# Attention's first head, late gates, late weights, merge weights and column sums rearranged

## The chip, the cores and the metric

One core of one Trainium2 chip runs one transformer block. Five engines work side by side, each through its own queue of instructions in order: TensorE (PE, with its weight loads PEld), VectorE (DVE), ScalarE (ACT), GpSimd (POOL) and SyncE (SP), which here only issues transfers; POOL issues some too. The metric is device time in microseconds of the whole program: before the change, the median of 3 runs is 1717.37 us (1715.96 to 1721.29).

## The reference

A block over 1024 tokens of width 1024, in float32: a modulated norm, a token mixer with two branches, and a convolutional feed-forward part. The mixer is what the change touches.

```python
proj = u @ w_in
p_fox, p_rwkv, p_gate = _split(proj, (FOX_COLS, RWKV_COLS, GATE_COLS))
...
o_fox = fox_attention(to_heads(q), to_heads(k), to_heads(v), log_f)    # 8 heads of 64, causal, softmax of
                                                                       # q k / 8 + cum_q - cum_k
o_rwkv = rwkv7_time_mix(p_rwkv, ...)
gate_fox, gate_rwkv = jnp.split(jax.nn.sigmoid(p_gate), N_BRANCHES, axis=-1)
merged = gate_fox * (o_fox @ fox_w_out) + gate_rwkv * (o_rwkv @ rwkv_w_out)
return merged @ w_o
```

After it come `h + gate1 * mix`, a second modulated norm whose shift and scale are columns of `silu(c) @ w_mod`, and the feed-forward part.

## The kernel before

**Products.** A float32 matrix is kept as two float32r parts, `hi` (a rounded copy) and `lo` (what is left). A product is hi hi + hi lo + lo hi, so a gate tile of 128 columns over 512 tokens is 3 x 8 = 24 matmuls of 128x128 by 128x512. `load_w` (line 243) loads a weight tile into `raw` and splits it into `hi` and `lo`: a cast on ACT and two subtractions on DVE, or, while `weave.late` is 1, a cast and four subtractions on POOL. `raw`, `whi` and `wlo` have two buffers each.

**Order.** PE's order is written out by hand for the whole kernel. The class `Weave` does this: it keeps a clock of its own (`now`), runs chains of generators when they are due, and in the time between takes products from a list of fillers (`step`, `fill`). `hold` keeps the filler back for a time, `use` keeps count of what ACT and DVE have to do. In attention (the block `manual_schedule` behind line 1021) DVE and ACT are also in program order; SP and POOL are ordered by a scheduler at build time, in the whole mixer. Transfers wait in the queue of the engine that issues them.

**Stages around the change.** The RWKV branch is worked through first, with `qk`, `v` and gate products (`gt`) as fillers. Its last steps are group norms in `head_sums` (products `mu` and `va` with the constant `blk_r`, splits `Ztr`, `Mtr`, `Zts`, `Mts` on ACT and POOL). When its pools `shp` and `rw` close, the pools `fxp` (eight tiles `h0` to `h7` of 4096 bytes a partition, for attention's output `fx`) and `at` (attention's tiles) open in the same memory, at addresses in the order in which tiles are first asked for. `shp` holds the constants `cst2`, the tiles `sh` and small columns; `blk_r` is the first tile of `rw`.

**Attention.** `load_head` brings one head from memory in three transfers on POOL's queue: `stA` (q and k, 2 x 128 rows), `stB` (their low parts and the decay sums, 2 x 68 rows) and `vh`. Three chains run: `s_chain` makes logits (`lg`, for each block of 128 queries: products with stA, stB and a causal mask), behind which `softmax` takes the row maximum (DVE, L1062), the exponential (ACT, L1066), and scales by the reciprocal of the sum (DVE, L1071 and L1072); `t_chain` transposes P (`tp`) and `halve` splits it into `th` (ACT) and `tl` (DVE, L1102); `a_chain` multiplies with v (`ov`), and `collect` adds the two halves (ACT L1133, DVE L1135) and splits a finished pair into `fx` (POOL L1142 and L1143, for the last head ACT and DVE). The fillers in this stage are the seven gate weights that are left, "late gates": two halves each, in one PSUM bank `rk_ps`. `gate_out` evicts a half: Abs and Relu from PSUM, Exp, Ln on ACT, an addition on DVE, Exp on ACT, then a write to `d_gate`. `s_chain` begins with a wait of 10,500 ns of the planner's clock, in which fillers run.

**Merge and output.** `br_open` loads and splits a merge weight (`raw_br`; `hi_br` on ACT, `lo_br` on POOL) in a pool `br` over attention's memory, `br_part` multiplies and applies the gates. Then `wo_mm` multiplies by `w_o`, eight steps `kt`. At `kt` 4 `mod_2` runs: 2 x 8 one-column products (`mps`; float32, so two matmuls each) that sum the columns for the second norm's shift and scale.

## Time and profile before

| | |
|---|---|
| runs | 1715.96, 1717.37, 1721.29 us |
| span of the profiled execution, first to last instruction | 1713.2 us (its own time is not listed) |
| mean granted clock of PE | 0.986 |
| late gate products `rk_ps` | 336 matmuls, 668.1 to 868.2 us from the span's start |
| first and last logits | 683.3 and 863.2 us |
| merge products `br` | from 877.6 us |
| output products `wo` | from 965.0 us |

Times in views are microseconds from the start of the span unless marked ns. A row of instructions gives the line, the engine, output and input tiles without buffer numbers, their shape and count; then busy time, mean ns of one, and idle time of that engine just before it with what ended most of it. The granted clock is the share of full speed that PE was given. L140 is the line of the helper that issues every matmul, so PE's work is told apart by tiles.

### The profile page before, as it was taken

How to read it: one execution, taken by the hardware profiler on the slowest of the kernel's cores; microseconds unless marked ns; L12 is line 12 of the kernel's file. 1: busy time of each engine (PE TensorE's matmuls, PEld its weight loads, DVE VectorE, ACT ScalarE, POOL GpSimd, SP SyncE). 2: the span in 40 equal slices, each digit the busy share in tenths (PEclk: the TensorE clock that was granted, in tenths of full speed). 3: DMA queues.
4: the chain of work that ended last, by engine and by line, in shares of the span. 5: the costliest groups of instructions: out<-in, count | busy, mean ns of one | idle time of the engine just before them, and what ended most of it. 6: DMA issues, size and time to landing. Idle time of an engine off the chain costs nothing.

```text
span 1713.2 us, 26506 instructions
## 1 busy us (share of the span) xinstructions
PE 1665.3 (97%) x9984; PEld 1367.0 (80%) x9984; DVE 1213.0 (71%) x2432; ACT 813.1 (47%) x1482; POOL 143.5 (8%) x175
## 2 busy tenths in 40 slices
PE   8899999999999999999999999999999999999998
PEld 7867777787777777888878888888888888888886
DVE  4576687777677632889777734897777777786677
ACT  5364343334344454766652314664444444454455
POOL 0001011111110002323212100000000000000000
PEclk9899999999999999999999999999999999999999
DMA  9287644533333226434268611132333223484463
GB/s 310 89 304 236 185 133 112 140 96 116 95 96 98 85 81 158 135 100 125 75 231 288 255 50 62 57 105 98 106 116 111 93 99 117 149 293 153 123 215 111
DMA packets 135311, 239.87 MB, mean 140 GB/s; under 512 B 39888, under 2 KB 64720, under 8 KB 135184
## 3 DMA queue, kind: packets, MB, share of 16 engines
q1 hardware_dynamic: 127232, 220.94, 39.8%
q0 software_dynamic: 7952, 17.25, 3.7%
q8 instruction: 78, 1.28, 0.3%
q14 instruction: 49, 0.40, 0.1%
HBM read 172.59 MB, written 65.54 MB: 139 GB/s over the span
## 4 chain that ended last, share of the span: by engine, by line
PE 80%; DVE 9%; DMA 4%; ACT 3%; SPq 2%; issue 1%; DVEq 0%; ACTq 0%; POOLq 0%
PE X L140 13%; PE D L140 12%; PE Y L140 6%; PE wo L140 5%; PE gt L140 5%; PE br L140 5%; PE ps_rkv L140 5%; PE qk L140 4%; PE rk_ps L140 4%; PE W L140 3%; PE lg L140 2%; PE ov L140 2%; PE tr L140 2%; PE sp L140 2%; PE tp L144 2%
## 5 line engine op out<-in xcount | busy, mean ns | idle before, releaser
L140 PE MATMUL D<-op,op 128*128 128x512 f32 x924 | 209.8, 389 | 0.0
L140 PEld LDWEIGHTS D<-op,op 128*128 128x128 f32 x924 | 173.3, 188 | 36.3 <-DVE op L1245 0.3
L140 PE MATMUL X<-T_m,S 128*128 128x512 f32 x440 | 107.3, 390 | 0.1
L140 PEld LDWEIGHTS X<-T_m,S 128*128 128x128 f32 x440 | 82.4, 188 | 18.2 <-ACT T_m L1670 0.6
L1244 ACT CAST op<-g 128x512 fp32r<-128x512 f32 x77 | 47.8, 621 | 73.0 <-PE D L140 47.9
L1245 DVE TENSOR_TENSOR op<-g,op 128x512 fp32r<-128x512 f32 x77 | 53.0, 689 | 40.9 <-ACT op L1244 40.8
L1481 DVE SCALAR_TENSOR_TENSOR c<-ab,vec,c 128x512 f32<-128x512 f32 x88 | 65.9, 749 | 19.5 <-ACT c L1484 17.9
L263 DVE TENSOR_TENSOR lo_in<-raw_in,hi_in 128x512 fp32r<-128x512 f32 x84 | 56.4, 706 | 31.6 <-PE gt L140 12.3
L796 DVE TENSOR_TENSOR t<-E,M 128x60 f32<-128x60 f32 (+24 forms) x248 | 56.8, 229 | 29.5 <-DMA M<-sm 24.2
L1445 DVE TENSOR_TENSOR S<-ur,S 128x512 fp32r<-128x512 f32 x66 | 45.5, 691 | 35.6 <-ACT S L1441 35.5
L261 ACT CAST hi_in<-raw_in 128x1024 fp32r<-128x1024 f32 x42 | 43.9, 1047 | 52.5 <-PE ps_rkv L140 17.2
L1441 ACT CAST S<-ur 128x512 fp32r<-128x512 f32 x66 | 41.0, 622 | 55.6 <-DVE ur L1434 30.6
L1445 DVE TENSOR_TENSOR A<-ur,A 128x512 fp32r<-128x512 f32 x64 | 44.0, 688 | 30.9 <-ACT A L1441 30.7
L140 PE MATMUL Y<-T_h,A 128*128 128x512 f32 x264 | 63.5, 389 | 0.0
L140 PE MATMUL Y<-T_h,S 128*128 128x512 f32 x264 | 63.3, 389 | 0.0
L140 PE MATMUL X<-B_b,A 128*128 128x512 f32 x252 | 60.8, 390 | 0.0
L140 PE MATMUL W<-B_f,A 128*128 128x512 f32 x252 | 60.6, 389 | 0.0
L1066 ACT ACTIVATE P<-lg,nm 128x896 f32<-128x896 f32 (+3 forms) x64 | 47.5, 744 | 22.1 <-DVE nm L1062 21.9
L140 PEld LDWEIGHTS Y<-T_h,A 128*128 128x128 f32 x264 | 49.6, 188 | 10.4
L798 DVE TENSOR_TENSOR E<-E,t 128x60 f32<-128x60 f32 (+24 forms) x248 | 53.7, 216 | 5.8
L140 PEld LDWEIGHTS Y<-T_h,S 128*128 128x128 f32 x264 | 49.5, 188 | 10.3
L1441 ACT CAST A<-ur 128x512 fp32r<-128x512 f32 x64 | 39.9, 623 | 34.2 <-PE X L140 31.5
(472 smaller groups left out, 4213.3 us busy)
## 6 DMA issues: line engine op xcount, KB each, us to landing
raw_in<-in_w_in SPq DMA_DIRECT2D x50, 512.0 KB, 3.7
wm<-in_w_mod SPq DMA_DIRECT2D x48, 512.0 KB, 6.5
ur<-in_w_up SPq DMA_DIRECT2D x44, 512.0 KB, 4.0
g<-d_g SPq DMA_DIRECT2D x35, 512.0 KB, 3.9
d_g<-gs SPq DMA_DIRECT2D x44, 256.0 KB, 2.0
d_g<-c SPq DMA_DIRECT2D x33, 256.0 KB, 4.4
d_st<-qh SPq DMA_DIRECT2D x64, 128.0 KB, 2.4
d_gate<-gs SPq DMA_DIRECT2D x32, 256.0 KB, 2.6
```

The lines of the kernel that those rows point to most:

```text
L140: nc.tensor.matmul(o, lhsT, rhs, start=start, stop=stop, skip_group_check=more)
L144: nc.tensor.transpose(o, i, eye)
L261: nc.scalar.copy(hi, raw)
L263: nc.vector.tensor_tensor(lo[:, c : c + NH], raw[:, c : c + NH], f32(hi[:, c : c + NH]), op=ALU.subtract)
L796: tt(tv, E32[:, 0:J, s : s + 1].to_broadcast([128, J, W]), M32[:, s : s + 1, s + 1 : 32].to_broadcast([128, J, W]), op=ALU.mult)
L798: tt(E32[:, 0:J, s + 1 : 32], E32[:, 0:J, s + 1 : 32], tv, op=ALU.add)
L1066: nc.scalar.activation(e[:, 0:n], lg[:, 0:n], AF.Exp, bias=nm[:, 0:1], accum_out=nm[:, 1:2])
L1244: nc.scalar.copy(hi, src)
L1245: tt(lo, src, f32(hi), op=ALU.subtract)
L1441: nc.scalar.copy(hi, src)
L1445: tt(lo, src, f32(hi), op=ALU.subtract)
L1481: stt(c, ab[:, x + hf * NH : x + hf * NH + NH], V("conv_w", 22 * x + i), c, op0=ALU.mult, op1=ALU.add)
```

## The change

Five edits. (1) The first head is loaded by `load_first`: five transfers into five `fxp` tiles in the order h3, h7, h2, h6, h5, and `s_chain` begins after 700 ns rather than 10,500; later heads keep `load_head`. (2) A late gate half is evicted by a tanh of half the product and an identity that halves it and adds 0.5, on ACT alone, with the ACT table set `exp_and_others` loaded ahead of attention and the one with Ln loaded behind it; the second half's output has a tile of its own (`gl`, two buffers). (3) Late weights are split like early ones, on ACT and DVE; POOL's subtraction for `fx` is issued in two pieces of 256. (4) The first two merge weights are loaded into `raw` and split (ACT, DVE) into gate-weight buffers before attention's pools close. (5) The column sums are taken four matmuls at a time between the output products of `kt` 3 to 7.

```diff
-    epsr = cp.tile([128, 3], F32, name="epsr")
+    epsr = cp.tile([128, 4], F32, name="epsr")
+    nc.vector.memset(epsr[:, 3:4], 0.5)
...
+        nc.scalar.copy(hi, raw)
         if weave.late == 1:
-            i = nc.gpsimd.tensor_copy(hi, raw)
-            if "head" in marks:
-                tc.add_manual_dep(i.ins, marks["head"].ins.name, NOSYNC)
-            for c in range(0, n, 256):
-                nc.gpsimd.tensor_tensor(lo[:, c : c + 256], raw[:, c : c + 256], f32(hi[:, c : c + 256]), op=ALU.subtract)
-        else:
-            nc.scalar.copy(hi, raw)
-            for c in range(0, n, NH):
-                nc.vector.tensor_tensor(lo[:, c : c + NH], raw[:, c : c + NH], f32(hi[:, c : c + NH]), op=ALU.subtract)
+            weave.use("ACT", weave.now, 900)
+            weave.use("DVE", weave.now, 1200)
+        for c in range(0, n, NH):
+            nc.vector.tensor_tensor(lo[:, c : c + NH], raw[:, c : c + NH], f32(hi[:, c : c + NH]), op=ALU.subtract)
...
+    def load_first():
+
+        parts = [d_st[0, 0], d_st[0, 1], d_st[0, 2, 0:68, :], d_st[0, 3, 0:68, :], d_v[0].rearrange("p a x -> p (a x)")]
+        tiles = [fxp.tile([128, S], F32R, tag=f"h{t}", name=f"first{t}") for t in (3, 7, 2, 6, 5)]
+        for t, x in zip(tiles, parts):
+            marks["head"] = nc.gpsimd.dma_start(t[0 : x.shape[0], :], x)
+        heads[0] = *tiles[0:4], tiles[4].rearrange("p (a x) -> p a x", x=128)
+
...
-    load_head(0)
+    load_first()
...
-            yield 10500
+            yield 700
...
-                A, B, _ = heads[h]
+                qa, ka, qb, kb, _ = heads[h]
...
-                        mm(lg[:, c0:c1], A[:, 0, qs], A[:, 1, c0:c1], start=True, stop=False)
+                        mm(lg[:, c0:c1], qa[:, qs], ka[:, c0:c1], start=True, stop=False)
...
-                        mm(lg[:, c0:c1], B[0:68, 0, qs], B[0:68, 1, c0:c1], start=False, stop=True)
+                        mm(lg[:, c0:c1], qb[0:68, qs], kb[0:68, c0:c1], start=False, stop=True)
...
-                    nc.gpsimd.tensor_tensor(fx[1][p][:, cs], o, f32(fx[0][p][:, cs]), op=ALU.subtract)
+                    for x in range(2):
+                        c = slice(cs.start + x * 256, cs.start + x * 256 + 256)
+                        nc.gpsimd.tensor_tensor(fx[1][p][:, c], o[:, x * 256 : x * 256 + 256], f32(fx[0][p][:, c]), op=ALU.subtract)
...
-                weave.hold = weave.now + 1000
+                weave.hold = weave.now + 700
...
-            g = gsp.tile([128, NH], F32, tag="sp0", name=f"gs{i}_{hf}")
-            m = at.tile([128, NH], F32, tag="gm", name=f"gm{i}_{hf}", bufs=1)
-            nc.scalar.activation(g, rk_ps, AF.Abs)
-            nc.scalar.activation(m, rk_ps, AF.Relu, scale=-1.0)
-            weave.hold = weave.use("ACT", weave.now, 960) + 210
-            nc.scalar.activation(g, g, AF.Exp, scale=-1.0)
-            nc.scalar.activation(g, g, AF.Ln, bias=1.0)
-            yield weave.use("ACT", weave.now, 960) + 140 - weave.now
-            tt(g, g, m, op=ALU.add)
-            yield weave.use("DVE", weave.now, 600) + 140 - weave.now
-            nc.scalar.activation(g, g, AF.Exp, scale=-1.0)
+            g = (at if hf else gsp).tile([128, NH], F32, tag="gl" if hf else "sp0", name=f"gs{i}_{hf}")
+            nc.scalar.activation(g, rk_ps, AF.Tanh, scale=0.5)
+            weave.hold = weave.use("ACT", weave.now, 480) + 210
+            nc.scalar.activation(g, g, AF.Identity, scale=0.5, bias=epsr[:, 3:4])
             weave.use("ACT", weave.now, 480)
...
+        nc.scalar.preload_act_table_set("exp_and_others")
         weave.run([a_chain(), t_chain(), s_chain()])
         weave.late = 2
         weave.run([drain()])
+    ahead = {}
+    for n in range(2):
+        raw = rp.tile([128, 1024], F32, tag="raw", name=f"raw_br0{n}")[:, 0:NH]
+        nc.sync.dma_start(raw, a["w_br"][n, :, 0:NH])
+        hi, lo = (wp.tile([128, 1024], F32R, tag=t, name=f"{t}_br0{n}")[:, 0:NH] for t in ("whi", "wlo"))
+        nc.scalar.copy(hi, raw)
+        nc.vector.tensor_tensor(lo, raw, f32(hi), op=ALU.subtract)
+        ahead[0, n] = hi, lo
+    use_ln_exp()
     es.close()
...
+        if (x, n) in ahead:
+            g = br.tile([128, S], F32, tag="g", name=f"g{x}_{n}")
+            nc.sync.dma_start(g, d_gate[8 * x + n])
+            opened[x, n] = ahead[x, n], g
+            return
...
+    sums2 = mod_2()
...
             wo_mm(t, kt, ps[t])
+            if kt > 2:
+                for _ in range(2):
+                    next(sums2, None)
         mg_split(1, kt)
-        if kt == 4:
-            for _ in mod_2():
-                pass
```

More of the change, by code (lines that the diff above doesn't have):

```diff
@@ L1011, in load_head @@
         vh = at.tile([128, 8, 128], F32R, tag="vh", name=f"vh{h}")
-        i = nc.gpsimd.dma_start(vh, d_v[h])
-        marks.setdefault("head", i)
-        heads[h] = A, B, vh
-    load_head(0)
+        nc.gpsimd.dma_start(vh, d_v[h])
+        heads[h] = A[:, 0, :], A[:, 1, :], B[:, 0, :], B[:, 1, :], vh
+    load_first()
     while len(weave.queue) > 12:
@@ L1115, in a_chain @@
                     yield from slot(ov_free)
-                vh = heads[h][2]
+                vh = heads[h][4]
                 order = [(0, th), (1, th), (1, tl), (0, tl)] if jj == I else [(0, th), (0, tl), (1, th), (1, tl)]
```

2 lines of the change are left out of this document (added).

## The prediction

> **What bounds the kernel now.** I read the page first, then a table by stage, then each stage's order of instructions.
>
> ```profile
> span 1713.2 us, 26506 instructions
> PE 1665.3 (97%) x9984; PEld 1367.0 (80%) x9984; DVE 1213.0 (71%) x2432; ACT 813.1 (47%) x1482; POOL 143.5 (8%) x175
> ```
>
> TensorE (PE) is busy for 97% of the span, so nothing this change does to other engines counts unless it closes a gap of PE or a stretch in which PE runs at a lower clock. The change touches the attention stage, the start of the merge and the output product; the table by stage (window, its length, busy time of PE, PEld, DVE, ACT, POOL, then the granted clock, DMA share, GB/s) shows where such gaps are.
>
> ```profile
> 668.00:690.00 22.00, 18.21 (x76) 14.29 (x75) 8.07 (x12) 9.59 (x17) 8.93 (x12) 0.92 0.81 187
> 690.00:740.00 50.00, 50.00 (x322) 44.66 (x320) 43.36 (x90) 36.76 (x88) 11.29 (x15) 1.00 0.46 139
> 740.00:760.00 20.00, 16.89 (x97) 14.30 (x97) 16.76 (x27) 11.42 (x25) 6.96 (x9) 0.91 0.43 121
> 840.00:860.00 20.00, 18.59 (x113) 16.07 (x112) 14.90 (x34) 13.83 (x34) 0.00 (x0) 1.00 0.04 14
> 860.00:880.00 20.00, 16.30 (x99) 13.87 (x99) 12.67 (x24) 13.43 (x28) 2.33 (x2) 1.00 0.34 116
> 979.00:990.00 11.00, 11.00 (x53) 9.47 (x52) 0.50 (x3) 0.00 (x0) 0.00 (x0) 0.69 0.20 81
> ```
>
> PE's gaps are the lengths less its busy time: 3.79, 3.11, 1.41 and 3.70 us, 12.0 in all. Three windows also have a low clock (0.92, 0.91, 0.69). Elsewhere in attention PE is full and DVE is at 43.36 of 50, so PE bounds it, with DVE close behind. The timeline (start, duration, engine, line, tiles, idle before in brackets) gives the causes; one line's own view (least, middle and longest duration in ns) and, from the chain of waits, what a 512-wide product takes at full clock and behind the column sums, follow it.
>
> ```profile
> 665.62 0.39 PE L140 MATMUL va<-Mts,blk_r 128*128 128x512 f32 x1
> 671.98 1.98 PE L140 MATMUL rk_ps<-u_hi,lo_in 128*128 128x512 f32 x8
> 676.28 0.60 ACT L1166 ACTIVATE gs<-rk_ps 128x512 f32<-128x512 f32 x1 [4.42 <-DMA d_gate<-gs]
> 677.42 3.32 PE L140 MATMUL rk_ps<-u_hi,hi_in 128*128 128x512 f32 x8 [3.47 <-ACT gm L1167]
> 680.54 2.42 PE L140 MATMUL rk_ps<-u_lo,hi_in 128*128 128x512 f32 x8
> 683.48 0.39 PE L140 MATMUL lg<-stA 128*128 128x512 f32 x1
> ...
> 746.18 1.29 POOL L1143 TENSOR_TENSOR fx<-o,fx 128x512 fp32r<-128x512 f32 x1
> 746.77 3.66 DVE L1072 TENSOR_SCALAR P<-P,nm 128x384 f32<-128x384 f32 x1
> 747.43 2.79 POOL L259 TENSOR_TENSOR lo_in<-raw_in,hi_in 128x256 fp32r<-128x256 f32 x4
> 750.94 0.45 PE L140 MATMUL ov<-th,vh 128*128 128x256 f32 x2 [2.21 <-DVE o L1135]
> 752.56 3.29 PE L140 MATMUL rk_ps<-u_hi,hi_in 128*128 128x512 f32 x8
> 755.65 1.25 PE L140 MATMUL rk_ps<-u_lo,hi_in 128*128 128x512 f32 x3
> ...
> 877.64 2.11 PE L140 MATMUL br<-fx,hi_br 128*128 128x512 f32 x8 [2.08 <-ACT hi_br L1218]
> ```
>
> ```profile
> L1072 DVE TENSOR_SCALAR P<-P,nm x64: 285/553/3658, 687.1 to 866.2; 128x896 f32<-128x896 f32 x8, 128x1024 f32<-128x1024 f32 x8, 128x128 f32<-128x128 f32 x8, 128x256 f32<-128x256 f32 x8
> ```
>
> ```profile
> 965.14 13.87 PE wo L140 x60
> 979.01 3.98 PE mps L140 x32
> 982.99 44.15 PE wo L140 x180
> ```
>
> First gap: the first late gate half ends its product, ScalarE (ACT) can't evict it because its output buffer is still being written to memory, and PE waits 3.47 us for the single PSUM bank. Then 16 products take 677.42 to 682.96, 5.5 us; at full clock, 13.87 / 60 = 0.231 each, they take 3.7: 1.8 us lost to the clock. Second gap: one scaling of P, of which the middle one takes 0.55, takes 3.66 and ends 0.2 us after the run of GpSimd (POOL) subtractions at 750.22. Behind it on DVE stands the eviction L1135 for which PE waits; then 11 rk_ps products take 752.56 to 756.75, 4.2 us for 2.5: 1.7 lost. Last gap: the merge's first weight, 2.08 of the 3.70.
>
> **The change, part by part.**
>
> *First head.* Before, planning puts 10,500 ns of gate product ahead of the first logits (683.48). Afterwards 700 ns, that is four rk_ps products: logits are asked for at about 668.13 + 4 x 0.23 = 669.05. Nothing is removed from PE; some 39 products (9 us) of cover move into attention. What is late next is the head itself.
>
> ```profile
> 661.41 1.29 POOL L707 TENSOR_TENSOR Mts<-ysq,Zts 128x512 fp32r<-128x512 f32 x1 [4.96 <-ACT Zts L706]
> 662.64 0.76 POOL L1008 DMA_DIRECT2D stA<-d_st  x1
> stA<-d_st POOLq DMA_DIRECT2D x1, 1024.0 KB, 5.3
> stB<-d_st POOLq DMA_DIRECT2D x1, 544.0 KB, 13.4
> DMA to landing us min/median/max: 15.7/15.7/15.7
> ```
>
> (The last three: a quiet pair of a later head, then the first stB.) Before, stA is issued right behind Mts on POOL's queue although what it overwrites was done earlier. I assume the new loads get the same place, five issues now, since their pool opens at the same point of the program. New tiles are laid out in the order in which they are asked for, from where the pools shp and rw began: h3 and h7 (q and k, first part) fill bytes 0 to 8192, h2 8192 to 12288. Pool shp is 4352 (cst2) + 2 x 2080 (sh) + 6 x 32 = 8704 bytes, and blk_r follows it: h2 lies over blk_r, which the va product reads until 665.62 + 0.39 = 666.0. So qb waits on POOL until then, and behind it in the queue kb, vh and all of head 1. In the quiet pair stA's 1024 KB land 5.3 us after issue and stB, issued behind stA's 0.76 of issuing, 13.4 after, some 8 us for 544 KB of 68 rows behind stA; half of it is 4. With 3 us of lead (half of stA's 5.3) qb lands at 666 + 7 = 673, kb beside it or 4 later. Bounds: no stall if the loads go ahead of Mts; 10 us if they land as stB did (663.39 + 15.7 = 679.1). I take 673.5, nearest the quiet rows: a stall of 4.5 in place of 3.79, **+0.7**. The clock then falls as it does now: 0. [...] The trace's second gap, whose longest idle piece is 2.21 us, fell to 0.91 all the same, so I keep the fall.
>
> *Gates and weights.*
>
> ```profile
> L1166 ACT ACTIVATE gs<-rk_ps 128x512 f32<-128x512 f32 x14 | 8.4, 602 | 5.8 <-DMA d_gate<-gs 4.4 <-PE rk_ps L140 1.4
> L1172 DVE TENSOR_TENSOR gs<-gs,gm 128x512 f32<-128x512 f32 x14 | 10.8, 769 | 12.9 <-ACT gs L1170 12.8
> L1174 ACT ACTIVATE gs<-gs 128x512 f32<-128x512 f32 x14 | 8.9, 636 | 1.0 <-DVE gs L1172 0.9
> L259 POOL TENSOR_TENSOR lo_in<-raw_in,hi_in 128x256 fp32r<-128x256 f32 x24 | 17.7, 765 | 5.5 <-PE rk_ps L140 5.5
> L261 ACT CAST hi_in<-raw_in x42: 1029/1047/1057, 55.8 to 654.9; 128x1024 fp32r<-128x1024 f32 x42
> L263 DVE TENSOR_TENSOR lo_in<-raw_in,hi_in x84: 636/684/1780, 56.9 to 657.4; 128x512 fp32r<-128x512 f32 x84
> L942 ACT ACTIVATE rs<-va,epsr x8: 680/687/700, 292.3 to 666.0; 128x512 f32<-128x512 f32 x8
> L197 ACT ACT_TABLE_LOAD x3 | 3.8, 1283 | 0.1
> ```
>
> A half's five ACT passes (the two that read PSUM at 0.60, the others at 0.636) become a tanh (0.60, as L1166 reads the same PSUM) and an identity with a bias column (0.69, as L942): 3.1 to 1.3 us, over 14 halves 25 us less. Six late weights (24 pieces of L259, four each) go from POOL to ACT (1.05 each, 6.3) and DVE (2 x 0.684, 8.2 in all, against 10.8 for the additions that go). ACT and DVE both end lighter, and the four long POOL runs go, so the 3.66 of L1072 falls to its like, and with it the 3.11 and the 1.7: **-4.8**. POOL keeps six fx subtractions, now in two pieces. The price is order: cast and subtractions stand in the hand-written queues of ACT and DVE, ahead of exponentials, P and tl. DVE waits there for the cast, PE for what is behind. Per weight that is 0 to 1.05 + 1.37 = 2.4 us; PE has gate products as cover in each such place, so I take 0.3: **+1.8** for six. Two table loads of 1.28 (L197) fall where PE stalls for the head and where it has merge products: 0. [...] The 1.41 at 840 to 860 I halve, since ACT, which has less to do, frees the banks there: **-0.7**.
>
> *Merge weights.* Two weights are loaded and split before attention's pools close, in buffers of the gates. The 2.08 goes (877.64); its cover is the last gate half and the last heads' products. The last 7 us of attention have no gate product left; with 9 us more of it I take 1.0 of the other 1.62: **-3.1**. Without that cover only the 2.08 goes.
>
> *Column sums.*
>
> ```profile
> 72.02 1.84 PE L140 MATMUL mod<-sc,wm 128*128 128x1 f32 x16
> 70.00:80.00 10.00, 10.00 (x71) 9.18 (x70) 5.76 (x17) 5.15 (x7) 0.12 (x1) 0.98 0.01 2
> ```
>
> The chain above shows 32 one-column products in one run. The 180 wo products behind them take 0.2453 each against 0.2312 ahead: 2.5 us, the 0.69 of the table. A run of 1.84 us (at 72) leaves the clock at 0.98, so runs of four, 0.46 us, should: **-2.5**. At 1.84 / 16 = 0.115 the 32 take 3.7 in place of 3.98, or more if their weight loads no longer overlap (+1.0); I take the row, **-0.3**.
>
> **Sum:** 0.7 - 4.8 + 1.8 - 0.7 - 3.1 - 2.5 - 0.3 = -8.9. Span 1713.2 - 8.9 = 1704.3. The median of the runs, 1717.37, is 4.2 over this span; the profiled execution's own time isn't shown, so I put 4.2 around it: **1708.5 us**, 0.5% faster.
>
> **Rivals.** *The head is in time.* For it: nothing holds the q and k tiles but cst2, done long before. Against: POOL's place and blk_r. The stall (4.5) and its clock (1.8) go: 1702.2. *The head comes as late as stB now.* For it: head 1 and, as the two buffers are free, head 2 crowd the same queue. Stall 10: 1714.0. *Split weights in the softmax's way,* the other side: every late weight stops PE for the whole 2.4 us, 14.5 in place of 1.8, which gives 1721.2; if the clock falls each time by 1.7 as at 752, 1731. It decides from (1.8 + 8.9) / 6 = 1.8 us a weight. For it: DVE is 87% busy at 690 to 740. Against: the additions that leave DVE are more than what comes. *The change doesn't do what it says:* cover runs out and the gaps come back at attention's end, so only the 2.08 and the column sums count: -4.9, 1712.5.
>
> **How the numbers follow.** Forecast 0.53, head in time 0.18, head late 0.10, split weights 0.11, gaps come back 0.08. The range goes from 1700 (head in time, and all small gaps too) to 1718 (head late and half a microsecond more per weight); outside lie the split weights and little else. Some 0.3% (5.2 us) is what these runs can tell from no change: below 1712.2 lie the forecast, the first rival and half of the last, 0.76; above 1722.5 the worse half of the split weights, 0.08.
>
> **What would show it.** Right: no POOL subtraction beside attention but fx, L1072 near 0.5 us, first logits near 669 with a wait on stB's successor of 3 to 6 us, merge starting without a wait for hi_br, wo at 0.231 throughout. Wrong: PE waits on hi_in or lo_in in attention, a first stall of 0 or over 8, or a clock below 0.95 at 965 to 1000.

## The result, and the profile after

The changed kernel takes 1728.61 us in the median of six runs (1726.29 to 1734.88), the kernel before 1717.99 in the median of the six beside them: a ratio of 1.007, 95% interval 1.0053 to 1.0087. The change makes the kernel slower by 0.7%. The forecast was 0.5% faster.

From the page of the changed kernel:

```profile
span 1725.6 us, 26447 instructions
PE 1665.6 (97%) x9984; PEld 1364.8 (79%) x9984; DVE 1206.9 (70%) x2433; ACT 808.4 (47%) x1453; POOL 118.3 (7%) x151
```

ACT, DVE and POOL are all busy for less time than before (813.1, 1213.0, 143.5), as the prediction said; the span is 12.4 us longer all the same. PE's busy time is the same, so the time went into waits.

Cut at the first instruction of each stage on PE (first late gate product, first merge product, first output product, first product behind it), the two profiles give:

| stage, us | before | changed | difference |
|---|---|---|---|
| ahead of the first late gate product | 668.35 | 666.38 | -1.97 |
| attention with late gates | 209.29 | 213.53 | +4.24 |
| merge | 87.34 | 98.24 | +10.90 |
| output product | 101.80 | 98.68 | -3.12 |
| from there to the end | 646.42 | 648.77 | +2.35 |
| span | 1713.2 | 1725.6 | +12.40 |

The first row varies from 666.4 to 676.9 over the profiles below, in which this stretch is the same program but for two table loads and a memset, mostly with the clock granted in it: from 100 to 640 us e11, at 674.2, was granted 0.98 and e9, at 667.9, 0.99, with the same shares ahead of that. So the experiments are read by the other rows, and "late part" below is all that follows the first late gate product: 1044.9 us before, 1059.2 in the changed kernel.

The table by stage for attention, merge and output product of the changed kernel (window, length, then busy time of PE, PEld, DVE, ACT, POOL, granted clock, DMA share, GB/s), with two short windows in attention:

```profile
666.38:879.91 213.53, 200.26 (x1201) 173.10 (x1200) 158.42 (x323) 126.56 (x280) 28.00 (x39) 0.98 0.37 107
879.91:978.15 98.24, 90.95 (x386) 74.22 (x384) 71.98 (x83) 25.82 (x40) 20.92 (x14) 0.97 0.78 278
978.15:1076.83 98.68, 98.68 (x482) 83.04 (x480) 40.27 (x68) 29.89 (x61) 0.00 (x0) 1.00 0.26 102
670.00:680.00 10.00, 9.91 (x36) 8.36 (x37) 4.66 (x10) 3.27 (x8) 0.43 (x1) 0.67 1.20 337
720.00:730.00 10.00, 10.00 (x62) 9.48 (x61) 8.03 (x18) 6.35 (x15) 2.19 (x4) 0.83 0.25 80
```

The same for the kernel before:

```profile
668.35:877.64 209.29, 197.10 (x1201) 171.73 (x1199) 164.52 (x324) 140.45 (x318) 49.87 (x62) 0.98 0.40 115
877.64:964.98 87.34, 87.34 (x385) 72.19 (x386) 70.41 (x82) 24.74 (x38) 23.37 (x16) 1.00 0.83 302
964.98:1066.78 101.80, 101.80 (x482) 85.51 (x481) 40.76 (x69) 27.59 (x59) 0.00 (x0) 0.97 0.25 99
```

The merge is the largest piece: PE never waited in it before, now it is idle for 98.24 - 90.95 = 7.3 us and loses some 3 to a lower clock. PE's timeline in the merge of the changed kernel (start, duration, what, idle before it and what ended that):

```profile
879.91 1.98 PE L140 MATMUL br<-fx,whi_br 128*128 128x512 f32 x8
...
889.89 1.07 PE L140 MATMUL br<-fx,wlo_br 128*128 128x512 f32 x4
894.32 3.06 PE L140 MATMUL br<-fx,hi_br 128*128 128x512 f32 x8 [3.36 <-ACT rk_m L1302]
...
906.00 1.07 PE L140 MATMUL br<-fx,lo_br 128*128 128x512 f32 x4
911.00 2.71 PE L140 MATMUL br<-fx,hi_br 128*128 128x512 f32 x8 [3.93 <-DVE mg_m L1315]
```

Four products are done by 890.96 and fill the four PSUM banks that the merge has in turn; then PE waits. The releaser named first, `rk_m`, is not it: that cast has nothing to do with the bank. What frees a bank is VectorE's multiplication by the gate, `mg_m`: the first ends at 893.49 + 0.69 = 894.18, and PE goes on at 894.32. VectorE's timeline in that place:

```profile
880.17 0.69 DVE L1195 TENSOR_TENSOR wlo_br<-raw_br,whi_br 128x512 fp32r<-128x512 f32 x1 [10.35 <-PE rk_ps L140]
890.72 0.75 DVE L1280 TENSOR_SCALAR acc<-wm,sc 128x1024 f32<-128x1024 f32 x1 [9.85 <-DMA wm<-in_w_mod]
892.29 1.28 DVE L1282 SCALAR_TENSOR_TENSOR acc<-wm,sc,acc 128x1024 f32<-128x1024 f32 x1 [0.82 <-DMA wm<-in_w_mod]
893.49 2.47 DVE L1315 TENSOR_TENSOR mg_m<-g,br 128x512 f32<-128x512 f32 x4
895.88 3.78 DVE L1303 TENSOR_TENSOR rk_m<-rk_raw,rk_m 128x512 fp32r<-128x512 f32 x6
901.98 2.24 DVE L1303 TENSOR_TENSOR rk_m<-rk_raw,rk_m 128x512 fp32r<-128x512 f32 x2 [2.31 <-ACT rk_m L1302]
904.14 6.12 DVE L1282 SCALAR_TENSOR_TENSOR acc<-wm,sc,acc 128x1024 f32<-128x1024 f32 x4
910.18 2.47 DVE L1315 TENSOR_TENSOR mg_m<-g,br 128x512 f32<-128x512 f32 x4
```

Two accumulations of column sums stand ahead of the first `mg_m`, and the tile they read, `wm`, comes late: VectorE waits 9.85 us for it. Then the second four `mg_m` stand behind eight splits of reference rows and four accumulations. And why `wm` is late, SP's queue shows:

```profile
880.89 0.33 SPq L1221 DMA_DIRECT2D raw_br<-in_w_br  x1
881.50 0.32 SPq L1175 DMA_DIRECT2D d_gate<-gs  x1
881.91 0.92 SPq L1226 DMA_DIRECT2D g<-d_gate  x2
883.00 0.86 SPq L1276 DMA_DIRECT2D wm<-in_w_mod  x2
```

The load of the fourth merge weight and the write of the last gate half stand ahead of the gate and the `wm` loads. (The third weight's load went out at 866.67, when the first weight's split had given its buffer back; two recorded texts below say "third" where the trace shows the fourth.) The fourth's load waits for a buffer that the second weight loaded ahead gives back at 880.86 (end of `wlo_br` above), and that split waits for the last late gate's products; the write waits for the last eviction. So `wm` is asked for 3.1 us *after* the first merge product. In the kernel before it was 2.1 us ahead of it, and VectorE's first multiplication came 3.5 us behind the first product:

```profile
872.74 2.60 SPq L1221 DMA_DIRECT2D g<-d_gate  x2
875.52 0.81 SPq L1260 DMA_DIRECT2D wm<-in_w_mod  x2
...
880.49 0.75 DVE L1264 TENSOR_SCALAR acc<-wm,sc 128x1024 f32<-128x1024 f32 x1 [2.69 <-DMA wm<-in_w_mod]
881.16 0.68 DVE L1299 TENSOR_TENSOR mg_m<-g,br 128x512 f32<-128x512 f32 x1
```

The 2.35 behind the output product is a third thing. ScalarE's timeline at the start of the kernel, at the first tanh and at the norm, and PE's behind the norm:

```profile
0.75 1.28 ACT L1185 ACT_TABLE_LOAD   x1 [0.75 <-PEq L1988]
2.03 1.28 ACT L198 ACT_TABLE_LOAD   x1
...
682.85 1.28 ACT L1171 ACT_TABLE_LOAD   x1
...
1080.93 1.28 ACT L284 ACT_TABLE_LOAD   x1
1082.22 0.30 ACT L284 ACTIVATE ssq<-ssq,epsr 128x4 f32<-128x4 f32 x1
1082.54 1.28 ACT L285 ACT_TABLE_LOAD   x1
...
1084.41 3.84 PE L140 MATMUL tr<-dg,h_sb 128*128 128x128 f32 x32 [1.90 <-DVE dg L1364]
```

The two new preloads (lines 1185 and 198) depend on nothing, so the build put both at the very start of ScalarE's queue, where they do nothing for attention. The first tanh loads its own table with a finished product waiting for it (1.28 at 682.85, PE idle for 0.99 up to 684.79), and the logarithm and the exponential of the norm load one each, with PE waiting 1.90. A load took 1.28 here, and the activation behind it started at once (1080.93 + 1.28 = 1082.21, start 1082.22).

### The profile page after: what moved, and what is told of

Read it like the earlier page. It is cut to its first block, busy times and chain, and to the rows that moved or that the text cites. A ratio compares the mean times of both kernels' runs of the same rounds, so it can differ in the third digit from the quotient of the medians.

```text
span 1725.6 us, 26447 instructions
## 1 busy us (share of the span) xinstructions
PE 1665.6 (97%) x9984; PEld 1364.8 (79%) x9984; DVE 1206.9 (70%) x2433; ACT 808.4 (47%) x1453; POOL 118.3 (7%) x151
## 3 DMA queue, kind: packets, MB, share of 16 engines
q8 instruction: 78, 1.28, 0.3%
## 4 chain that ended last, share of the span: by engine, by line
PE 73%; DVE 12%; DMA 6%; ACT 5%; issue 3%; SPq 2%; POOL 0%; DVEq 0%; ACTq 0%; POOLq 0%
PE X L140 13%; PE D L140 12%; PE Y L140 6%; PE gt L140 5%; PE wo L140 5%; PE br L140 4%; PE ps_rkv L140 4%; PE W L140 3%; PE rk_ps L140 3%; PE qk L140 2%; PE ov L140 2%; PE lg L140 2%; PE sp L140 2%; DVE t L793 1%; PE tp L144 1%
## 5 line engine op out<-in xcount | busy, mean ns | idle before, releaser
L140 PE MATMUL D<-op,op 128*128 128x512 f32 x924 | 209.8, 389 | 0.0
L260 DVE TENSOR_TENSOR lo_in<-raw_in,hi_in 128x512 fp32r<-128x512 f32 x96 | 64.4, 706 | 38.5 <-ACT hi_in L255 12.3
L255 ACT CAST hi_in<-raw_in 128x1024 fp32r<-128x1024 f32 x48 | 50.2, 1047 | 51.7 <-PE ps_rkv L140 16.7
L1106 DVE TENSOR_TENSOR tl<-tp,th 128x512 fp32r<-128x512 f32 (+1 forms) x80 | 49.8, 633 | 13.8 <-ACT th L1103 13.1
L140 PEld LDWEIGHTS Y<-T_h,A 128*128 128x128 f32 x264 | 49.6, 188 | 10.3
L140 PEld LDWEIGHTS Y<-T_h,S 128*128 128x128 f32 x264 | 49.6, 188 | 10.3
```

The costliest lines, as they stand in the source:

```text
L140: nc.tensor.matmul(o, lhsT, rhs, start=start, stop=stop, skip_group_check=more)
L255: nc.scalar.copy(hi, raw)
L260: nc.vector.tensor_tensor(lo[:, c : c + NH], raw[:, c : c + NH], f32(hi[:, c : c + NH]), op=ALU.subtract)
L1106: tt(tl[:, 0:w], tp[:, 0:w], f32(th[:, 0:w]), op=ALU.subtract)
```

## The experiments

Sixteen kernels. "Stages" gives attention, merge, and what follows the output product, in us from the profile; the output product took 98.68 in all sixteen. Ratios are to the kernel before in the same session, with 95% intervals.

| | stages | late part | ratio |
|---|---|---|---|
| before | 209.3, 87.3, 646.4 | 1044.9 | 1 |
| changed | 213.5, 98.2, 648.8 | 1059.2 | 1.0070 [1.0053, 1.0087] |
| e1 | 209.7, 98.4, 646.5 | 1053.3 | 1.0038 [1.0027, 1.0050] |
| e2 | 216.3, 89.4, 651.2 | 1055.6 | 1.0019 [1.0007, 1.0031] |
| e3 | 204.3, 95.5, 650.3 | 1048.8 | 1.0008 [0.9993, 1.0022] |
| e4 | 202.9, 87.2, 646.6 | 1035.3 | 0.9931 [0.9911, 0.9951] |
| e5 | 210.6, 87.2, 646.5 | 1043.0 | 0.9977 [0.9960, 0.9993] |
| e6 | 208.9, 92.6, 646.5 | 1046.8 | 0.9994 [0.9975, 1.0012] |
| e7 | 212.7, 87.2, 646.5 | 1045.1 | 0.9990 [0.9977, 1.0003] |
| e8 | 209.8, 87.3, 646.5 | 1042.4 | 0.9984 [0.9966, 1.0001] |
| e9 | 198.6, 87.2, 646.5 | 1031.0 | 0.9907 [0.9888, 0.9925] |
| e10 | 203.4, 87.2, 646.5 | 1035.8 | 0.9944 [0.9922, 0.9966] |
| e11 | 207.0, 94.7, 646.5 | 1046.9 | 0.9995 [0.9979, 1.0012] |
| e12 | 206.3, 87.2, 646.5 | 1038.7 | 0.9950 [0.9936, 0.9965] |
| e13 | 209.6, 94.1, 646.1 | 1048.5 | profile only |
| e14 | 209.7, 88.8, 646.1 | 1043.3 | profile only |
| e15 | 201.1, 87.2, 646.5 | 1033.4 | profile only |
| e16 | 204.4, 87.2, 647.0 | 1037.3 | 0.9937 [0.9916, 0.9959] |

**e1, the table preloads tied to their places.**

```diff
-        nc.scalar.preload_act_table_set("exp_and_others")
+        i = nc.scalar.preload_act_table_set("exp_and_others")
+        tc.add_manual_dep(i.ins, marks["act"].ins.name, NOSYNC)
...
-    use_ln_exp()
+    use_ln_exp(marks["act"])
```

> The changed kernel with both preloads of an activation table tied behind the ScalarE instruction that they follow in the text (the last gate's exponential, the last late gate's second pass), nothing else. In the changed kernel both stand at the start of ScalarE's queue (0.75 and 2.03 us), the first tanh loads its own table at 682.85, and the norm after the output product loads four (1080.93, 1082.54 and two more), with PE idle for 1.90 us at 1082. Theory 1 (the preloads do nothing where they are wanted): no table load at the norm and the gap of 1.90 gone, so the stage from the end of the output product to the end of the kernel goes from 648.8 to about 646.4, and the gap of 0.99 at 684 closes: 1725.6 to about 1722. Rival (the norm waits for DVE anyway, the loads hide): that stage stays at 648 or more, and the time within 1 us. The merge (first merge product to first output product, 98.4) stays in both.

(`marks["act"]` is the last ScalarE instruction of a gate written so far.) The stage behind the output product went from 648.77 to 646.54, the value of before: theory 1. Attention went from 213.5 to 209.7 as well, but not through the tables: the 0.99 at 684 went and a 1.25 for an exponential came at 677. What went is clock. Over attention of the changed kernel, in windows of 4 us, PE's busy time times one less the granted clock comes to 4.8 us; in e1 it is 0, with the same stalls nearly:

```profile
671.00:681.00 10.00, 8.72 (x47) 7.30 (x48) 7.18 (x15) 6.29 (x13) 0.68 (x2) 1.00 1.25 303
718.00:728.00 10.00, 10.00 (x69) 9.10 (x68) 9.48 (x21) 7.79 (x18) 3.07 (x4) 1.00 0.30 87
```

So attention is compared below with this loss taken off where there is one. Attention without it is 0.9 longer in e1 than in the changed kernel (209.7 against 208.7).

**e2, no merge weights ahead.** `ahead` stays empty, and the two weights go the old way.

> The changed kernel without the two merge weights loaded ahead (they are loaded and split in the merge, on ScalarE and GpSimd, as in the kernel before). Theory A (the merge stalls because the last gate halves end later and their write stands ahead of the merge's loads on SP's queue): the merge stays at 95 us or more, and 2 us for the first weight come on top. Theory B (the merge stalls because, with the weights ahead, the build lays out VectorE's merge work in another order, with the multiplications by the gate in fours behind eight reference splits and four accumulations): the order goes back to nearly that of before, the gap of 3.93 at 907 goes and that of 3.36 at 891 shrinks, the merge takes 88 to 91, and the kernel 1718 to 1720.

The merge took 89.4, and the build's order on VectorE went back to nearly that of before. That was as theory B had it; but the wait of 1.99 for the first weight, now counted into attention, and one of 1.83 are part of the bargain, so the two stages together are 6.0 shorter than in the changed kernel. Behind the output product this profile took 651.2 and that of e3 650.3, against 648.8 in the changed kernel with its gap of 1.90 at the norm; that the clock fell there is my estimate, from the 1.7 or 3.4 us that a fall costs in the two kernels' traces.

**e3, gate products ahead of the first logits again.** In `s_chain`, `yield 10500` for `yield 700`.

> The changed kernel with 10500 in place of 700 ns of late gate product ahead of the first logits, all else as in the changed kernel (first head in its own tiles, weights ahead). The build's order then has 45 gate products ahead of the first logits and 28 behind the last, in place of 4 and 72. Theory A (late gate tail): the last gate write comes some 8 us earlier against the first merge product, the merge falls to 88 to 91. Theory B (VectorE's order, which is the same in fours here): the merge keeps at least one stall of 3 to 4, 93 or more. For attention: if the early start of the head is what gains, attention (213.5 from the first late gate product to the first merge product) gets longer by 2 to 4; if the gate products are better spent at the start, it gets shorter by 2 to 4 since PE's stall for the first head (2.42) is covered and the halves of the tail no longer wait for their one bank (1.08, 0.69).

The merge stayed at 95.5 with stalls of 1.32 and 5.12, against theory A as I had put it then: the gate write had only moved with the merge. Attention took 204.3, with no loss of clock, against 213.5 - 4.8 = 208.7: the early first head costs 4.4.

**e4, e1 with the late weights split on GpSimd.** The branch of `load_w` that the change takes out is put back.

> As e1 (tables tied), with the late weights split on GpSimd as before. To be compared with e1. Theory 1 (the split stands in the way of the softmax on VectorE, where it waits 1 to 2 us for the cast: 709.01 gap 1.55, 782.49 gap 0.58, 818.40 gap 0.60): attention is 3 us or more shorter than in e1. Theory 2, that of the prediction (the GpSimd subtractions hold VectorE's scaling for 3 us and PE behind it): a scaling of P of over 2 us is back and attention is longer than in e1 by up to 5 us.

Attention 202.9, 6.8 less than e1, and no long scaling came back: one scaling of P took 1.33 at most (line 1079 in e4, line 1072 in the kernel before):

```profile
L1079 DVE TENSOR_SCALAR P<-P,nm x64: 285/554/1334, 676.3 to 842.9; 128x896 f32<-128x896 f32 x8, 128x1024 f32<-128x1024 f32 x8, 128x128 f32<-128x128 f32 x8, 128x256 f32<-128x256 f32 x8
```

So attention goes the way of theory 1, and not that of the prediction's price for the second gap. The merge, which neither theory had touched, went to 87.2. PE's timeline and SP's queue between attention and merge of e4 say why:

```profile
861.29 1.98 PE L140 MATMUL gt<-u_hi,hi_in 128*128 128x512 f32 x8
...
872.17 1.98 PE L140 MATMUL br<-fx,whi_br 128*128 128x512 f32 x8
...
862.87 0.32 SPq L1178 DMA_DIRECT2D d_gate<-gs  x1
863.28 0.91 SPq L1230 DMA_DIRECT2D g<-d_gate  x2
864.38 0.82 SPq L1280 DMA_DIRECT2D wm<-in_w_mod  x2
```

Here the planner gets six gates done beside attention, not seven. The seventh runs behind it on two banks of its own, 10.9 us, and `wm` is asked for 7.8 us ahead of the first merge product.

**e5, e1 with a gate kept back by hand.**

```diff
     weave.late = 1
+    held = weave.queue.pop()
...
         weave.run([drain()])
+        weave.queue.append(held)
+        weave.prefetch()
```

> As e1 (tables tied, late weights split on ScalarE and VectorE, merge weights ahead), but the last gate item is taken out of the queue ahead of attention and run between attention and merge, its weight loaded as soon as attention has ended: six gates run beside attention and 48 gate products (10.9 us in e4) stand between the last late gate's write and the first merge product. Theory A (what stalls the merge is that its loads stand on SP's queue behind the last gate write, which comes 1.6 us after the first merge product in e1 and the changed kernel, 5.3 ahead of it in the kernel before): the merge goes from 98.4 to 87 to 88, with no gap over 0.5, though the weights stay ahead and VectorE still splits. Rival (the weights ahead, or the split on VectorE, spoil the merge by themselves): the merge stays above 93. Attention with the kept gate inside (first late gate product to first merge product): if the split on VectorE is what costs, 206 to 210 as in e1 against 202.9 in e4; if the tail of gate products on one bank is what costs, 203 to 205. Time: 1708 to 1714 by theory A.

The merge took 87.2 with no stall, with the weights ahead and the split on VectorE as in e1: theory A in the form that counts, the lead of the loads over the first merge product (`wm` is asked for 8.7 us ahead of it). The build's order on VectorE is another as well, though: two accumulations, not four, stand between the first four multiplications and the next. So e5 alone doesn't part the lead from the order; e6, e13 and e14 do. Attention: 210.6, less 3.3 of clock and less 2.4 for the kept weight, which the hold makes late: 204.9, against 202.9 in e4. So of the 6.8 between e1 and e4 some 2 are the split, and the other 4.7, between e1 and e5, come with the gate left over.

**e6, VectorE's order in the merge tied.** A dependency from each split of reference rows and each accumulation on the multiplication ahead of it in the text.

> As e1, with an order tied on VectorE in the merge: the splits of the reference rows and the accumulations of column sums may not be put ahead of the multiplication by the gate that precedes them in the text (the build's order becomes two splits, four accumulations, two multiplications, two splits, two multiplications, in place of eight splits, four accumulations, four multiplications). If VectorE's order alone makes the second stall (3.93 at 908), it falls below 1.5 and the merge takes 93 to 95 with the first stall (2.82) still there: 1716 to 1718 in the profile. If the loads on SP's queue are what is late (theory A), the order makes no difference to the first stall, and the second only moves, since the accumulations wait for their loads: merge 96 to 99, 1719 to 1722.

The merge took 92.6, with 1.7 lost to the clock: the second stall went from 3.93 to 0.15, the first stayed (3.12). The order makes the second stall, not the first.

**e7, e5 with 10500 ns of cover ahead.**

> As e5, with 10500 ns of gate product ahead of the first logits in place of 700. With six gates in attention the build then has 45 gate products ahead of the first logits and none behind the last. If an early first head gains by itself, e7 is 2 to 6 us slower than e5. If the gate products at the start are worth as much as those at the end (they only move), within 1.5. If they are worth more at the start, as e3 against the changed kernel suggests (attention 204.3 against 213.5), 2 to 5 faster. I hold the first, since nothing is left for the gaps between the last heads, which were 3.5 in the kernel before with 12 products behind the last logits.

2.1 slower in attention than e5, and 4.0 with the clock losses (3.3 in e5, 1.4 in e7) taken off: gaps of 0.3 to 1.3 at 856 to 868, where no gate product was left. Cover can be spent too early as well as too late.

**e8, the kernel before with the column sums moved and nothing else.**

> The kernel before with nothing changed but the column sums' 32 one-column products, which go two at a time behind the output products from the fourth on in place of all in one run. Prediction's step: 2.5 us of clock and 0.3 of product time, so the output-product stage goes from 101.8 to 99.0; in the changed kernel and e1 to e4 it took 98.68. If the clock falls for another reason in that place, it stays at 101 or more. Nothing else moves, 1710 to 1711 in the profile.

The output product took 98.68 at a clock of 1.00, the rest stayed (over its ten runs the gain is at the edge of what can be told from none, see the table); and a scaling of P took 3.67, as in the kernel before. From e8's table by stage:

```profile
971.38:1070.06 98.68, 98.68 (x481) 83.04 (x480) 40.57 (x68) 27.60 (x59) 0.00 (x0) 1.00 0.26 102
```

And from the view of that one line (least, middle and longest duration in ns):

```profile
L1072 DVE TENSOR_SCALAR P<-P,nm x64: 285/553/3668, 692.8 to 872.6; 128x896 f32<-128x896 f32 x8, 128x1024 f32<-128x1024 f32 x8, 128x128 f32<-128x128 f32 x8, 128x256 f32<-128x256 f32 x8
```

**e9, e4 with 5000 ns of cover.**

> As e4 (tables tied, late weights on GpSimd, a gate left over behind attention by itself) with 5000 in place of 700 ns of gate product ahead of the first logits: 24 products instead of 4. The first head's stall (2.29 at 673 in e4, first logits asked for at 670.2, second part landed at 672.9) ends while PE has cover to about 674, so it goes; what the cover lacks later is at most 20 products of those 62 behind the last logits, which hid nothing there. If products are worth more at the start: attention 200.5 to 201.5 against 202.87 in e4, merge 87.2 as there. If they only move: 202 to 203.5.

The best of all: 1701.15 us, ratio 0.9907 [0.9888, 0.9925], faster than both kernels. Attention of e9:

```profile
667.91:866.55 198.64, 192.91 (x1201) 169.56 (x1200) 153.45 (x312) 125.44 (x279) 52.84 (x70) 1.00 0.45 126
```

PE is idle for 5.7 us in it; in e4 for 9.8, before for 12.2. The first head's stall is gone and later gaps are shorter.

**e10, e4 with the fx subtraction in one piece.**

> As e4, with the fx subtraction on GpSimd in one piece of 512 columns (1.29 us) as in the kernel before in place of two of 256. In the kernel before a scaling of P took 3.66 us beside a run of one such subtraction and four of a late weight; in e4 the longest scaling takes 1.33 though the weights are split on GpSimd too. If the size of the piece is what lets VectorE in, a scaling of over 2.5 us is back and attention is 2 to 5 us longer than e4's 202.87. If the place of the runs changed (the scaling no longer meets them), or if it is GpSimd's work as such, the longest scaling stays under 1.6 and attention within 1 us of 202.87. The prediction took the run of all five as one; I hold the second likelier (0.6).

The longest scaling took 1.72, attention 203.4, within 0.6 of e4. So the size of the piece isn't what cured the second gap. Nor are meetings of a scaling with GpSimd's subtractions gone: they still hold it up, in e1 even without a late weight on GpSimd (2.06 for a 128x128, of which the shortest takes 0.29):

```profile
769.90 2.06 DVE L1076 TENSOR_SCALAR P<-P,nm 128x128 f32<-128x128 f32 x1
770.42 1.44 POOL L1149 TENSOR_TENSOR fx<-o,fx 128x256 fp32r<-128x256 f32 x2
```

What is met only in the kernel before and in e8 is one scaling with both runs in a row, the fx subtraction and the four of a late weight (746.77 in the prediction's rows, 3.66); in the other kernels a scaling meets one or the other.

**e11, e4 with the old gates.**

> As e4 without the tanh: late gates by the five old passes, no change of table, weights on GpSimd, first head early, merge weights ahead. The build leaves no gate over behind attention here, and has VectorE's merge work in the order that stalls (four multiplications, eight splits of reference rows, four accumulations around, four multiplications). Theory A (the lead of the merge's loads over the first merge product): merge 94 to 99 although neither the split on VectorE nor the tanh is there. If it were the split on VectorE that spoils the merge: 87 to 88. Attention (it has a gate more inside on the one bank than e4): if the tanh is worth what its passes save, 207 to 212, with waits on the gate's write buffer back; if it is worth nothing, 203 to 205.

Without the tanh the build leaves no gate over, and the merge stalls (0.59 and 3.80, 94.7), though the weights are split on GpSimd: the split on VectorE isn't needed for the stalls. The lead is missing here too, `wm` is asked for 4.4 us after the first merge product. Attention took 207.0, with waits on the gate's buffer up to 1.57. But 3.1 of it is clock, which leaves 203.9, 1.0 more than e4 with a gate more inside: that is the branch in which the tanh is worth nothing to attention.

**e12, e4 with 10500 ns and a gate kept back.**

> As e4 with 10500 ns ahead of the first logits, and the last gate item held back by hand as in e5, since the build doesn't leave it over here: 45 products ahead of the first logits, 14 behind the last, 48 of the kept gate. If products at the start are worth more, attention 200 to 202 like e9 or less; if cover is then missing between the last heads (as in e7, where gaps of 0.3 to 1.3 came back at 852 to 868 and attention was 2.1 longer than in e5), 203 to 206. A wait for the kept gate's weight of 2 to 2.5, as in e5 (2.37) and e7 (2.50), comes with the hand-made hold and is to be taken off. Merge 87.2.

Attention 206.3, or 201.6 without the hold's wait of 2.5 and the 2.2 that the clock lost around it (0.88 and 0.78 at 850 to 870), with a gap of 2.14 at 856 near its end: less than e4, more than e9. Between 700 and 10500, 5000 is better than either.

**e13, e1 with the last gate's writes on GpSimd's queue; e14, also the merge weights' loads from the third on held behind `wm`.**

```diff
-            nc.sync.dma_start(d_gate[i, :, cs], g)
+            (nc.gpsimd if i == 15 else nc.sync).dma_start(d_gate[i, :, cs], g)
...
-        nc.sync.dma_start(raw, a["w_br"][n, :, x * NH : x * NH + NH])
+        i = nc.sync.dma_start(raw, a["w_br"][n, :, x * NH : x * NH + NH])
+        if "wm" in last:
+            tc.add_manual_dep(i.ins, last["wm"].ins.name, NOSYNC)
...
+                last["wm"] = i
```

> As e1, with the two writes of the last gate issued from GpSimd's queue. On SP's queue the load of the third merge weight then still stands ahead of the loads of gate 0 and of the first two modulation tiles; it waits for a buffer that is free only when the second weight loaded ahead has been split, which waits for the last late gate's products (880.86 in the changed kernel, 0.95 after the first merge product). If the last gate write is what holds the loads: they are issued 4 us or more ahead of the first merge product, the first stall (2.82 in e1) goes and the merge takes 92 to 95. If the third weight's load holds them as well: they are issued within a microsecond of the time in e1 against the first merge product, the first stall stays between 1.5 and 3 and the merge at 95 to 99.

> As e13, and the load of the third and later merge weights may not be put ahead of the modulation tiles of its step on SP's queue. Nothing that waits for the last gate then stands ahead of the merge's loads. Queue theory: they are issued 4 us or more ahead of the first merge product, the first stall goes; the second depends on VectorE's order, which is again four multiplications, eight splits, accumulations, four multiplications: 0 to 4; merge 88 to 93 in place of 98.4. If the loads are late for another reason (the memory that they are loaded into is freed late), they are issued no earlier than in e1 and the merge stays at 95 or more.

In e13 the loads went out right behind the fourth weight's load, 1.4 us after the first merge product (at 883.92) in place of 2.0 in e1: that load holds them as well. The first stall went nevertheless, which neither branch had: the build now put one accumulation ahead of the first multiplications, not two, and the first `mg_m` came at 893.93, just inside the 10.9 us that four banks give. The second stall was 3.80, the merge 94.1. SP's queue in e13:

```profile
884.90 0.33 SPq L1222 DMA_DIRECT2D raw_br<-in_w_br  x1
885.28 0.90 SPq L1227 DMA_DIRECT2D g<-d_gate  x2
886.36 0.82 SPq L1277 DMA_DIRECT2D wm<-in_w_mod  x2
```

And in e14, where the first merge product starts at 877.55:

```profile
866.67 0.88 SPq L1230 DMA_DIRECT2D g<-d_gate  x2
867.73 0.81 SPq L1279 DMA_DIRECT2D wm<-in_w_mod  x2
```

9.8 us of lead, no first stall, a second of 1.35, a merge of 88.8. The queue theory holds, and both instructions are blockers: the load by e13, the write by e2, where the gate's loads go out right behind it (885.78 behind 885.36). VectorE's order up to the second multiplications is that of e13, so between these two only the lead differs: 94.1 to 88.8, of which 3.0 is clock. From e1 to both, one accumulation has moved as well.

**e15, e4 with the cast on ScalarE.**

> As e4, with the late weights' cast on ScalarE (1.05 us, in its written order) and the subtractions on GpSimd. e4 took 202.9 for attention, e1 209.7 and e5 208.2 without its wait for the kept weight (2.4). If VectorE is what is in the way (it waits for the cast and then subtracts for 1.3), attention is 202 to 204.5. If the cast on ScalarE holds exponentials and copies of tp, 206 to 209. A gate is left over behind attention as in e4, so the merge takes 87.2.

Attention 201.1, less than e4 itself. ScalarE has room for the cast; what is in the way when the split stands there is VectorE, waiting for the cast and then subtracting.

**e16, all causes taken away together.**

> The changed kernel with all the causes taken away at once: tables tied (e1), late weights cast on ScalarE and subtracted on GpSimd (e15), 5000 ns of cover ahead of the first logits (e9), the last gate's writes and the third weight's load out of the way on SP's queue (e14), VectorE's order in the merge tied (e6). The build leaves no gate over behind attention here, so the merge is bare as in the changed kernel. If the causes are all of it: merge 87.2 to 88 with no stall over 0.5, attention 198 to 200 with the two evictions of the tail (1.08, 0.69) back, from the first late gate product to the end 1031 to 1033 us, against 1031.0 in e9, 1044.9 in the kernel before and 1059.2 in the changed one. If something else stalls the merge: 91 or more there.

The merge took 87.20 with no gate left over: the queue and the order are all of its loss. Attention was missed, 204.4 with 1.7 of it clock (0.83 at 730 to 740): with a seventh gate inside, it has waits of up to 1.39 that e9 doesn't have. The late part is 1037.3 against 1031 to 1033 expected, so the edits don't simply add up in attention, where each moves the planner's order.

## Why the prediction was wrong, step by step

The span came out 21.3 us above the 1704.3 of the sum: merge 10.9 (forecast 0 but for its first wait), attention 10.3 (+4.2 for -6.1), behind the output product 2.4, less 0.3 in the output product and the 2.0 ahead of the change. The time, 1728.6, lies where the rival of the split weights had it (1721 to 1731), by luck: the split cost 2 to 4 us, and most of the miss is elsewhere.

**Merge weights, -3.1: the step that failed.** The 2.08 did go: the merge's first product starts without a wait. But the step costed only the wait that it removed, and took as cover the last gate half and the last heads' products. What it didn't ask is who else needs that time. The loads of the merge stand on SP's queue; the last late gate held them up, directly by its write and indirectly by the weights ahead, whose buffers it occupies. With the heads' work no longer behind the last gate (before: last gate write 872.31, merge 877.64; changed: 881.50 and 879.91) that lead went from 5.3 us to -1.6. Measured: +10.9, of which 3.36 and 3.93 are stalls and 3.4 is clock behind them. From e1's 98.4, clearing SP's queue brings the merge to 88.8 (e14), tying VectorE's order to 92.6 (e6), both to 87.2 (e16). No rival had it. "What is late next" was answered for PE's queue and never for SP's.

**First head, +0.7.** The mechanism was right: `first` waits on GpSimd's queue for the `va` product (2.54, up to 664.33), kb and qb come late, and the stall was 2.42 (1.8 to 3.1 in the experiments with the early start), not 4.5: within its bounds of 0 and 10, below the 3 to 6 that was to show it right. "The clock then falls as it does now: 0" isn't sure: it fell in 4 of the 11 profiles with this start, and in the changed kernel's for 3.3 us in place of 1.7. What failed is "some 39 products of cover move into attention" at no cost. They moved to its end, where they ran on one bank with waits of 1.08 and 0.69 for the eviction; e3 and e9 put the early start at 4.2 to 4.4.

**Second gap, -4.8.** The gap of 3.11 and its clock did go (longest scaling 1.28 in the changed kernel). But e4, e10 and e15 keep the subtractions on GpSimd and don't have it either, so it wasn't bought by moving them. That GpSimd's subtractions hold a scaling up was right and still is so (1.28 at 821.59 in the changed kernel, beside a subtraction at 821.26; 2.06 in e1); a meeting with two runs in a row, in one schedule, was taken for the price of that work. And other waits came in its place: attention has 13.3 us of idle PE, against 12.2 before.

**Split weights, +1.8.** The place was named rightly ("DVE waits there for the cast, PE for what is behind"). VectorE's and PE's timeline at the first of them in the changed kernel:

```profile
706.07 1.29 DVE L260 TENSOR_TENSOR lo_in<-raw_in,hi_in 128x512 fp32r<-128x512 f32 x2 [2.09 <-ACT hi_in L255]
707.40 0.96 DVE L1066 TENSOR_REDUCE nm<-lg 128x1 f32<-128x768 f32 x1
708.28 1.28 DVE L1106 TENSOR_TENSOR tl<-tp,th 128x512 fp32r<-128x512 f32 x2
...
709.01 0.39 PE L140 MATMUL ov<-tl,vh 128*128 128x256 f32 x1 [1.55 <-DVE tl L1106]
```

VectorE stands for 2.09, splits for 1.29, and PE waits 1.55 for the `tl` behind. The price is about 2 by e5 against e4 and 3.9 by e5 against e15, nearer the 1.8 than the rival's 14.5. What the step left out is the planner: with the split on VectorE it has seven gates inside attention, in e4 and e15 six, and the seventh is what leaves the merge bare. That is worth more than the split: 11.2 in the merge and 4.7 in attention (e1, e4, e5). The split isn't all that decides it, since e11 and e16 subtract on GpSimd and have seven as well.

**Table loads, 0.** Wrong, through "two table loads": the preloads floated to the start and became one load in the way at the first tanh and four at the norm, of which two (1080.93, 1082.54) held PE up and two (1029.08, 1030.69) fell beside output products: +2.2 (e1).

**Column sums, -2.8.** Right: -3.12, and e8's profile has it alone.

**The 1.41 and the tail, -0.7 and -1.0.** The gaps at 840 to 860 went (idle 0.27), the same time came back as the tail's 1.08 and 0.69.

The ledger of attention is -6.1 by these steps; measured +4.2 in the changed kernel, -6.4 in e4 and -10.7 in e9.

## What to carry to other kernels

Work that is moved out of the end of a stage was the lead of the next stage's loads: list what stands on the loading queue ahead of them, and when each of those is released, before costing the move. An instruction that the build may place freely, such as a table preload, is where its dependencies put it and not where the text has it. When an engine is relieved, ask what the planner does with the room.

## What the runs showed of the hardware

The clock fell behind a stall in one profile and not behind the same stall in the next. From the first late gate product to the end of the output product each fall in the traces of the two kernels lasted 3.41 or 6.83 us at half clock, so it costs 1.7 or 3.4 us of full work: in the changed kernel the granted clock is 0.50 from 721.06 to 724.47 and from 669.86 to 676.69, and for 3.41 from 895.14 and from 912.20; in the kernel before for 3.41 from 678.00 and from 753.10 and for 6.83 from 981.79. The lower shares given above are means over longer windows. The pair of waits of 1.55 within 12 us (709 and 719 in the changed kernel) is in seven of these profiles at the same place of the schedule: in three (changed, e2, e5) the clock fell in the 10 us behind, to 0.83 to 0.92 in the mean over 10 to 20 us, 1.4 to 1.7 us lost, in four (e1, e6, e13, e14) it stayed at 1.00. Behind the first head's stall it fell at 2.10, 2.42 (changed), 3.00 and 3.06 and not at 1.81, 1.90 (e13), 2.12, 2.29 (e4, e15), 2.44 and 2.51 (e14); in the changed kernel that fall was the one to 0.67 for 10 us, 3.3 us. A forecast that puts 1.7 behind a stall of 2 us should give it a chance (4 of 11 profiles here), not a certainty.
